# Weight units of 1024 columns in place of 512 in a two-layer diffusion trunk

## The chip, the core and the metric

The kernel runs on one core of one Trainium2 chip. The metric is the device time of one execution in microseconds, and shorter is better. The engines are named as the profile names them: PE is TensorE (matrix products), PEld its weight loads, DVE is VectorE, ACT is ScalarE, POOL is GpSimd, SP is the engine whose queue issues most DMAs here.

## What is computed

Two layers of a transformer trunk over 256 latent tokens and 256 context tokens, model width 1024. Cut to what matters:

```python
for l in range(2):
    ux = modulate(rms_norm(x, norm1_g[l]), sx1, cx1)      # same for the context h
    qa, ka, va, qb, kb, vb, pc, gates = project(ux, w_in[l], ...)
    ya = neighborhood_attention(...)   # branch a, 6 heads
    yb = gqa_block_attention(...)      # branch b, 6 query and 2 key heads, rotary
    yc = multiscale_pool(pc, ...)      # branch c
    m = ga * (ya @ w_br_a) + gb * (yb @ w_br_b) + gc * (yc @ w_br_c)
    x = x + gx1 * (m @ w_out[l])
    u2 = modulate(rms_norm(x, norm2_g[l]), sx2, cx2)
    x = x + gx2 * ((silu(u2 @ w_ff1[l]) * (u2 @ w_ff3[l])) @ w_ff2[l])   # width 2816
    # the context stream h gets the same, in the first layer only
```

The modulation vectors (`sx1`, `cx1`, ...) are products of `silu(c)` with `w_mod[l]`. All is in 32-bit floats.

## The kernel before

**Products in parts.** Each operand of a large product is held as a high and a low part, and a product is three matmuls: high by high, high by low, low by high (`mm3`, L228 to L230). A weight therefore passes three hands: a DMA on the SP queue brings it into a buffer `raw`; ACT copies it, rounded, to `wh` (L134); DVE subtracts to make `wl` (L146). PE can begin a block of products when `wh` is there and needs `wl` one or two matmuls later.

**Units.** The weights come as a list of units in the order of their use, each 128 partitions by at most `UNIT` = 512 columns: two row blocks (of 128 rows) by 256 columns, or one row block by 384 columns for the projections of branch a and of the queries of branch b. The class `Weights` keeps 7 `raw` buffers, and 6 each of `wh` and `wl` (`RAW`, `SPLIT`). When a job takes a unit (`get`), units up to 4 behind it are given to DVE to split, one more to ACT, and a DMA is issued for each `raw` buffer that a split frees.

**Special units.** 32 units of the first modulations come into slots of a general pool `gp` (68 slots of 2 KB a partition): 16 are used as they come ("whole"), 16 are split ("far"). Some jobs treat the two streams (latent, context) one after the other: the last two column pairs of `w_out` and `w_ff2` and the first pair of `w_ff1`/`w_ff3`, in layer 0. Their units are kept from the first stream for the second, with the parts in slots of `gp` ("keep"; `kept`).

**Jobs and order.** The main line is a list of jobs (`program`): first products woven with the first modulation, projections (`chunk_job`, `pool_job`), merges of the branches (`merge_job`), `w_out` and `w_ff2` (`into_job`), `ff_job`, and in the last layer `ff_first`, whose products start before the norm is known. `P`, `Q`, `N` name the pool, query and branch-a projections that open layer 1. Attention, norms and transposes are side work, woven a step at a time between steps of the main line; the later modulations are background work (`mod_bg`: DMAs to `mraw`, products summed in `macc` on DVE, L495 to L501, and for some of them on POOL, L498 and L499). A norm is: squares (`sq` on ACT, `ssq` on DVE, L520), the sum on PE (`ss`, L537, with its parts `ssh` and `ssl`), `rs` and `rstd` (L543 to L546), then `ut` (L566, L579) and its parts `uh` (ACT) and `ul` (DVE, L581). A scheduler then sets each engine's final order from dependences and program order; every engine runs its queue in order, so an instruction that waits holds all behind it.

Of the kernel before, what the change touches and what calls it, by code (L numbers as in the profile page):

```python
# [19 lines left out]
UNIT = 512  # L20
# [76 lines left out]
class Weights:  # L97
    """Weights in the order of their use: loaded far ahead, split a few units ahead."""

    RAW = 7  # L100
    SPLIT = 6
# [7 lines left out]
    def _dma(self, lim):  # L109
        while self.n_dma < min(lim, len(self.specs)):  # L110
            i = self.n_dma
            if self.specs[i][2:] in (("whole",), ("far",)):
                raw = self.slot([P, UNIT], name="whole")
            else:
                raw = self.pool.tile([P, UNIT], F32, tag="raw", bufs=self.RAW, name=f"raw{i}")
            for fill in self.specs[i][1]:
                fill(self.nc.sync, raw)
            self.raw[i] = raw
            self.n_dma += 1

    def part(self, i, tag):
        if self.specs[i][2:] == ("keep",):
            return self.slot([P, UNIT], F32R, name=tag)
        return self.pool.tile([P, UNIT], F32R, tag=tag, bufs=self.SPLIT, name=f"{tag}{i}")

# [27 lines left out]
    def whole(self, i):  # L153
        """Units that are used as they come."""
# [8 lines left out]
    def get(self, cols, held=0):  # L163
        """The next unit; `held` units before it are still to be used."""
        i = self.n_get
        self._dma(self.n_lo + self.RAW)
        self._lo(i + self.SPLIT - 1 - held)
        self._dma(self.n_lo + self.RAW)
        self._hi(min(i + self.SPLIT - held, self.n_lo + self.RAW))
# [6 lines left out]
class Trunk:  # L176
    def __init__(self, ctx, tc, a, out):
        self.nc, self.tc, self.a, self.out = tc.nc, tc, a, out
        self.cp = ctx.enter_context(tc.tile_pool(name="cp", bufs=1))
        self.gp = ctx.enter_context(tc.tile_pool(name="gp", bufs=68))  # L180
# [27 lines left out]
    def gT(self, T, name):  # L208
        """(high, low) tiles of T tokens; the two share a slot where they fit."""
# [15 lines left out]
    def mm3(self, out, st, mv, start, stop):  # L225
        """out += st.T @ mv, both operands as (high, low) parts."""
# [29 lines left out]
    def setup(self):  # L256
# [22 lines left out]
        # silu(c), silu(c_ctx) as columns, whole and in two parts  # L279
# [23 lines left out]
    def load_x(self, h):  # L303
        """Half of the channels of both streams."""
# [25 lines left out]
    def rows(self, l):  # L330
        """Per-channel vectors of a layer, turned from rows into columns."""
# [19 lines left out]
    def layer_consts(self, l):  # L351
        """Tables of a layer: rotary with the gains, relative bias, pooling weights."""
# [5 lines left out]
        tab = self.g([P, 2, 2, 2, HD], name="rope")  # q/k, tile, cos/sin  # L358
# [22 lines left out]
    def load_bias(self, l, head):  # L381
        """rpb (columns reversed) of a head: a run per query that covers its four key rows."""
# [10 lines left out]
    def mod_first(self, l, j):  # L393
        """Modulation from whole weights, four passes a product: TensorE has nothing else to do."""
# [72 lines left out]
    def mod_loads(self):  # L467
        """The weights of the jobs of mod_bg, in their order."""
# [9 lines left out]
    def mod_bg(self):  # L478
        """Modulation on VectorE: products summed over the row blocks, then over partitions."""
# [53 lines left out]
    def norm_rstd(self, c):  # L533
        """1 / rms of the tokens c, on every partition."""
# [13 lines left out]
    def need_u(self, kt, sl):  # L548
        """Emits the normed activations up to here."""
# [4 lines left out]
    def norm_u(self, kts, vs):  # L554
        """u = rmsnorm(x) * g * (1 + scale) + shift, as (high, low) parts."""
# [30 lines left out]
    def chunk_job(self, l, kind, p=0, fresh=False):  # L586
        wi = self.a["w_in"][l]
        cols = 256 if kind == "kb" else 384
        kpu = UNIT // cols
# [20 lines left out]
        def run(get):  # L610
# [12 lines left out]
            per = 2 // kpu  # L623
            for i0 in range(0, nu, per):
                ws = [get(cols, i) for i in range(per)]
                todo = [(i, k, tt) for tt in range(ntt) for i in range(per) for k in range(kpu)]
                if fresh:
                    todo.sort()
                for n, (i, k, tt) in enumerate(todo):
                    kt = (i0 + i) * kpu + k  # L630
                    step(ws[i], kt, k, tt)
                    if kt == KT - 1:
                        self.chunk_evac(l, kind, st, tt, ps[tt])
                    if n % 2 == 1:
                        yield
                if fresh and i0 + per == nu // 2:
# [55 lines left out]
    def q_stacks(self, srcs, scale):  # L692
        """Heads A and B of a pair: their (high, low) parts stacked on partitions."""
# [60 lines left out]
    def rotate(self, eng, z, nh, i, tt):  # L754
        """z (normed, nh heads) times gain, then rotary."""
# [80 lines left out]
    def pv(self, yps, y, h, n, v, pts):  # L836
        """The head's values, its (high, low) parts stacked on the stationary side, times both parts of P."""
# [108 lines left out]
    def unit(self, w, k0, nk, c0):  # L946
        """nk row blocks from k0 of 256 columns from c0."""
# [9 lines left out]
    def units(self, w, c0, nkt=KT, k0=0):  # L957
        return [self.unit(w, k0 + k, min(2, nkt - k), c0) for k in range(0, nkt, 2)]

    def kept(self, sl, specs, run):  # L960
        """A job on one stream of two: the units that the first one takes are kept for the second."""
# [15 lines left out]
    def pair(self, get, rhs, sl, ps, done, fresh=False):  # L977
        """Two column tiles of the tokens sl; done(c) as soon as tile c is complete."""
        nkt = len(rhs)
        nu = -(-nkt // 2)  # L980
        for i in range(nu):
            w = get(256)
            nk = w[0].shape[1]
            for c in range(2):
                for k in range(nk):
                    kt = 2 * i + k
                    if rhs is self.uu:
                        self.need_u(kt, sl)
                    self.mm3(
                        ps[c][:, sl],  # L990
                        [x[:, k, c * P : (c + 1) * P] for x in w],
                        [x[:, sl] for x in rhs[kt]],
                        kt == 0,
                        kt == nkt - 1,
                    )
# [516 lines left out]
```

## Time and profile before

| what | value |
|---|---|
| three runs | 1279.52, 1279.59, 1282.94 us |
| median | 1279.59 us |
| span of the profiled execution | 1281.1 us |
| PE busy | 1224.6 us, 96% |
| DVE busy | 951.9 us, 74% |
| ACT busy | 654.8 us, 51% |
| POOL busy | 315.4 us, 25% |
| moved by DMA | 185.5 MB, 145 GB/s on the mean |

The profiled execution is 1.5 us longer than the median; all places below are given in microseconds from its start. The rough map: 0 to 60 the first modulation and first products, to 180 projections and the start of attention in layer 0, to 420 attention and merges, to 500 `w_out` and the norms of the second half, to 840 the feed-forward part of layer 0, to 1080 layer 1 up to `w_out`, to the end the feed-forward part of layer 1. PE is busy nearly throughout, so what matters is the 56.5 us in which it is not, and what it waits for there.

### The profile page before, as it was taken

To read this page: it belongs to the slowest core of one execution; us is meant where nothing else is said; L and a number is where in the kernel's file an instruction comes from. 1 tells how busy PE (TensorE), PEld (TensorE's weight loads), DVE (VectorE), ACT (ScalarE), POOL (GpSimd) and SP (SyncE) were. 2 spreads that over 40 slices of the span, in tenths; PEclk is the share of its full clock that TensorE was granted. 3 is DMA by queue.
4 is the path that set the end of the run, shared out by engine and by line. 5 is a ranking of instruction groups with operands and counts; after the bars stand their busy time and mean duration, and the time that the engine had idled before them with its cause. 6 is when DMAs were issued, how large, how long until landed. Compare 5 with 4: busy or idle time off the path is not lost.

```text
span 1281.1 us, 21486 instructions
## 1 busy us (share of the span) xinstructions
PE 1224.6 (96%) x7415; PEld 1088.4 (85%) x7415; DVE 951.9 (74%) x1781; ACT 654.8 (51%) x1421; POOL 315.4 (25%) x335
## 2 busy tenths in 40 slices
PE   7999999899998979999999999989999999899998
PEld 2788888677786878888888888989999999899998
DVE  5867788998899888775555565597878878755563
ACT  4656578465432363333222333465888767654553
POOL 3252443755767530000000000067011100100000
PEclk9899999999999889999999999999999999999999
DMA  8632334434444544555455555325244466566663
GB/s 285 199 80 67 89 110 105 134 108 125 135 157 147 162 119 131 165 173 175 162 175 170 175 171 163 114 49 138 85 108 108 147 188 182 156 183 183 184 184 100
DMA packets 176137, 185.52 MB, mean 145 GB/s; under 512 B 14121, under 2 KB 149917, under 8 KB 176029
## 3 DMA queue, kind: packets, MB, share of 16 engines
q1 hardware_dynamic: 174220, 181.50, 46.5%
q0 software_dynamic: 1808, 2.66, 1.9%
q8 instruction: 58, 0.95, 0.3%
q14 instruction: 51, 0.41, 0.1%
HBM read 183.05 MB, written 1.05 MB: 144 GB/s over the span
## 4 chain that ended last, share of the span: by engine, by line
PE 73%; DVE 11%; ACT 5%; issue 4%; DMA 3%; POOL 3%; SPq 1%; DVEq 0%; ACTq 0%; POOLq 0%
PE acc L228 22%; PE acc L229 22%; PE acc L230 22%; DVE wl L146 3%; DMA whole<-in_w_mod_dram 2%; PE y L843 2%; ACT wh L134 1%; DVE macc L501 1%; DMA mraw<-in_w_mod_dram 1%; ACT p L832 1%; PE pt L889 1%; PE modt L508 1%; PE s L866 1%; DVE ptl L240 1%; POOL mt L498 1%
## 5 line engine op out<-in xcount | busy, mean ns | idle before, releaser
L134 ACT ACTIVATE wh<-raw 128x512 fp32r<-128x512 f32 (+2 forms) x512 | 307.2, 613 | 358.6 <-PE acc L229 267.0
L146 DVE TENSOR_TENSOR wl<-raw,wh 128x512 fp32r<-128x512 f32 (+2 forms) x512 | 365.7, 722 | 164.0 <-ACT wh L134 158.6
L228 PE MATMUL acc<-uh,wh 128*128 128x256 f32 (+1 forms) x1104 | 373.4, 338 | 6.4 <-DVE b L1249 3.6
L230 PE MATMUL acc<-uh,wl 128*128 128x256 f32 (+1 forms) x1104 | 369.5, 335 | 2.5 <-DVE wl L146 2.5
L229 PE MATMUL acc<-ul,wh 128*128 128x256 f32 (+1 forms) x1104 | 369.6, 335 | 0.3 <-DVE ul L581 0.3
L228 PEld LDWEIGHTS acc<-uh,wh 128*128 128x128 f32 x1104 | 211.7, 192 | 27.2 <-issue 3.8
L230 PEld LDWEIGHTS acc<-uh,wl 128*128 128x128 f32 x1104 | 211.3, 192 | 23.5 <-DVE wl L146 2.7
L229 PEld LDWEIGHTS acc<-ul,wh 128*128 128x128 f32 x1104 | 211.6, 192 | 19.8 <-DVE ul L581 0.7
L501 DVE SCALAR_TENSOR_TENSOR macc<-mraw,sf,macc 128x512 f32<-128x512 f32 x168 | 140.7, 849 | 58.7 <-DMA mraw<-in_w_mod_dram 57.8
L566 POOL TENSOR_TENSOR ut<-xT,rstd 128x256 f32<-128x256 f32 x30 | 25.2, 870 | 435.6 <-DVE rstd L546 435.5
L228 PE MATMUL acc<-wh,uh 128*128 128x384 f32 (+1 forms) x304 | 100.3, 330 | 4.6 <-ACT uh L1313 4.4
L229 PE MATMUL acc<-wl,uh 128*128 128x384 f32 (+1 forms) x304 | 98.2, 323 | 4.2 <-DVE wl L146 4.2
L230 PE MATMUL acc<-wh,ul 128*128 128x384 f32 (+1 forms) x304 | 98.7, 325 | 0.0
L499 POOL TENSOR_TENSOR macc<-macc,mt 128x512 f32<-128x512 f32 x56 | 84.3, 1506 | 3.2
L228 PE MATMUL acc<-hh,wh 128*128 128x512 f32 (+1 forms) x216 | 75.9, 352 | 0.0
L230 PE MATMUL acc<-hh,wl 128*128 128x512 f32 (+1 forms) x216 | 75.6, 350 | 0.0
L229 PE MATMUL acc<-hl,wh 128*128 128x512 f32 (+1 forms) x216 | 75.5, 350 | 0.0
L498 POOL TENSOR_SCALAR mt<-mraw,sf 128x512 f32<-128x512 f32 x56 | 63.1, 1129 | 40.6 <-DMA mraw<-in_w_mod_dram 26.5
L228 PEld LDWEIGHTS acc<-wh,uh 128*128 128x128 f32 x304 | 59.0, 194 | 6.1 <-ACT uh L1313 4.5
L229 PEld LDWEIGHTS acc<-wl,uh 128*128 128x128 f32 x304 | 59.1, 194 | 5.5 <-DVE wl L146 4.5
L832 ACT ACTIVATE p<-s,m 128x512 f32<-128x512 f32 (+1 forms) x72 | 44.3, 621 | 29.8 <-PE acc L229 8.7
L230 PEld LDWEIGHTS acc<-wh,ul 128*128 128x128 f32 x304 | 58.8, 193 | 0.6 <-DVE ul L1315 0.4
(278 smaller groups left out, 2327.5 us busy)
## 6 DMA issues: line engine op xcount, KB each, us to landing
raw<-in_w_ff_dram SPq DMA_DIRECT2D x264, 256.0 KB, 3.0
mraw<-in_w_mod_dram SPq DMA_DIRECT2D x160, 256.0 KB, 3.1
raw<-in_w_in_dram SPq DMA_DIRECT2D x112, 256.0 KB, 2.8
raw<-in_w_in_dram SPq DMA_DIRECT2D x144, 64.0 KB, 2.0
whole<-in_w_mod_dram SPq DMA_DIRECT2D x32, 256.0 KB, 5.5
raw<-in_w_out_dram SPq DMA_DIRECT2D x32, 256.0 KB, 3.0
raw<-in_w_in_dram SPq DMA_DIRECT2D x16, 192.0 KB, 2.8
raw<-in_w_br_c_dram SPq DMA_DIRECT2D x8, 256.0 KB, 2.9
```

Of the source, the lines that this page charges most:

```text
L134: self.nc.scalar.activation(hi[:, :n], self.raw[i][:, :n], AF.Copy)
L146: self.nc.vector.tensor_tensor(lo[:, :n], self.raw[i][:, :n], self.hi[i][:, :n].bitcast(F32), ALU.subtract)
L228: mm(out, st[0], mv[0], start=start, stop=False)
L229: mm(out, st[0], mv[1], start=False, stop=False)
L230: mm(out, st[1], mv[0], start=False, stop=stop)
L240: self.late.append(lambda: nc.vector.tensor_tensor(lo, src, hi.bitcast(F32), ALU.subtract))
L498: nc.gpsimd.tensor_scalar(t, w, c, 1.0, ALU.mult, ALU.mult)
L499: nc.gpsimd.tensor_tensor(acc[v], acc[v], t, ALU.add)
L501: nc.vector.scalar_tensor_tensor(acc[v], w, c, acc[v], ALU.mult, ALU.add)
L566: eng.tensor_tensor(ts[i][:, 0, :], self.xT[:, kt, c], self.r0[:, c], ALU.mult)
L832: nc.scalar.activation(pt, ps, AF.Exp, scale=-1.0, bias=m, accum_out=s[:, 0:1])
L843: mm(o, st, t[:, kt % 2, :], start=kt == 0 and i == 0, stop=kt == n - 1 and i == 1)
```

## The change

`UNIT` becomes 1024, with `RAW` = 3 and `SPLIT` = 4. A unit is now four row blocks by 256 columns, or two by 384 (768 columns; for the last row blocks of an odd count, less). Whole, far and kept units stay at 512 columns (`HALF`), since they lie in `gp` slots; the pool falls from 68 to 65 slots. `per` chooses two row blocks a unit for a job on one stream of two. `get` loses its argument `held`. Each loop walks a unit in two halves, so the order of products within a job is the same.

Columns held or under way, in units of ordinary jobs: before 7 x 512 in `raw` and 6 x 512 in parts, after 3 x 1024 and 4 x 1024. In the kept jobs, whose units stay at 512 columns, a job that takes a unit has 2 further units given to DVE instead of 4, and 3 `raw` buffers instead of 7.

```diff
-UNIT = 512
+UNIT = 1024
+HALF = UNIT // 2
...
-    RAW = 7
-    SPLIT = 6
+    RAW = 3
+    SPLIT = 4
...
-                raw = self.slot([P, UNIT], name="whole")
+                raw = self.slot([P, HALF], name="whole")
...
-            return self.slot([P, UNIT], F32R, name=tag)
+            return self.slot([P, HALF], F32R, name=tag)
...
-    def get(self, cols, held=0):
+    def get(self, cols):
         i = self.n_get
         self._dma(self.n_lo + self.RAW)
-        self._lo(i + self.SPLIT - 1 - held)
+        self._lo(i + self.SPLIT - 1)
         self._dma(self.n_lo + self.RAW)
-        self._hi(min(i + self.SPLIT - held, self.n_lo + self.RAW))
+        self._hi(min(i + self.SPLIT, self.n_lo + self.RAW))
...
-        self.gp = ctx.enter_context(tc.tile_pool(name="gp", bufs=68))
+        self.gp = ctx.enter_context(tc.tile_pool(name="gp", bufs=65))
...
-        kpu = UNIT // cols
+        kpu = {256: 4, 384: 2}[cols]
...
-            per = 2 // kpu
-            for i0 in range(0, nu, per):
-                ws = [get(cols, i) for i in range(per)]
+            for i in range(nu):
+                w = get(cols)
+                for k0 in range(0, kpu, 2):
...
-    def units(self, w, c0, nkt=KT, k0=0):
-        return [self.unit(w, k0 + k, min(2, nkt - k), c0) for k in range(0, nkt, 2)]
+    def units(self, w, c0, nkt=KT, k0=0, per=4):
+        return [self.unit(w, k0 + k, min(per, nkt - k), c0) for k in range(0, nkt, per)]
+
+    def per(self, sl):
+
+        return 4 if sl.stop - sl.start == self.tokens else 2
...
-            wu = [rows(0, 2), rows(2, 1)]
+            wu = [rows(0, 3)]
...
-        return self.kept(sl, self.units(w, jp * 256, nkt, k0), run)
+        return self.kept(sl, self.units(w, jp * 256, nkt, k0, self.per(sl)), run)
...
-            ws._dma(ws.n_whole + 4 + 2 * KT)
+            ws._dma(ws.n_whole + 2 + 2 * KT)
...
-                    ws._lo(ws.n_whole + 4)
+                    ws._lo(ws.n_whole + 2)
```

Over the whole program DVE's queue falls from 1742 to 1511 listed rows and ACT's from 1333 to 1096; PE's products are the same. Three places on DVE, where the order around a norm moves:

First pair of `w_ff1`/`w_ff3` of layer 0, latent stream, behind the norm of the context stream. Its eight kept units before are 5092, 5110, 5128, 5146, 5368, 5386, 5404 and 5448, so `wl_5448` is the eighth and last; the rows stand from the end of the first four norm steps on.

```order
L581 TENSOR_TENSOR ul_5174<-ut_5426,uh_5173 128x256
L581 TENSOR_TENSOR ul_5176<-ut_5428,uh_5175 128x256
L146 TENSOR_TENSOR wl_5448<-raw_5094,wh_5408 128x512
L579 TENSOR_SCALAR ut_5430<-ut_5430,A_111,mod_109 128x256
L579 TENSOR_SCALAR ut_5434<-ut_5434,A_111,mod_109 128x256
L581 TENSOR_TENSOR ul_5178<-ut_5430,uh_5177 128x256
L581 TENSOR_TENSOR ul_5180<-ut_5434,uh_5179 128x256
L509 TENSOR_REDUCE mod_109<-modt_5592 128x4
```

The same place of the changed kernel, where the eight units are 4744, 4762, 4984, 5002, 5020, 5064, 5096 and 5122:

```order
L582 TENSOR_TENSOR ul_4790<-ut_5042,uh_4789 128x256
L582 TENSOR_TENSOR ul_4792<-ut_5044,uh_4791 128x256
L147 TENSOR_TENSOR wl_5064<-raw_4986,wh_5024 128x512
L580 TENSOR_SCALAR ut_5046<-ut_5046,A_111,mod_109 128x256
L580 TENSOR_SCALAR ut_5050<-ut_5050,A_111,mod_109 128x256
L582 TENSOR_TENSOR ul_4794<-ut_5046,uh_4793 128x256
L582 TENSOR_TENSOR ul_4796<-ut_5050,uh_4795 128x256
L510 TENSOR_REDUCE mod_109<-modt_5208 128x4
L510 TENSOR_REDUCE mod_109<-modt_5214 128x4
L147 TENSOR_TENSOR wl_5096<-raw_5004,wh_5068 128x512
L460 TENSOR_TENSOR mod_109<-mod_109,cols_108 128x8
L147 TENSOR_TENSOR wl_5122<-raw_5022,wh_5100 128x512
```

Behind the first norm steps there is now the sixth unit of eight where there was the eighth, and the last two stand behind two reduces that wait for PE (`modt`).

Start of layer 1, DVE, at the norm of the context stream: the eight units of the `Q` job before are 8860, 8878, 8898, 8944, 8992, 9018, 9022 and 9049.

```order
L146 TENSOR_TENSOR wl_8898<-raw_8526,wh_8884 128x384
L240 TENSOR_TENSOR ssl_8835<-ssq,ssh_8834 128x256
L146 TENSOR_TENSOR wl_8944<-raw_8544,wh_8904 128x384
L543 TENSOR_SCALAR rs_8915<-ss_8912 128x256
L146 TENSOR_TENSOR wl_8992<-raw_8562,wh_8950 128x384
L545 SCALAR_TENSOR_TENSOR rs_8916<-rs_8916,rs_8915 128x256
L546 SCALAR_TENSOR_TENSOR rstd_8622<-rs_8916,rstd_8622 128x256
L146 TENSOR_TENSOR wl_9018<-raw_8580,wh_8998 128x384
L566 TENSOR_TENSOR ut_8922<-xT,rstd_8622 128x256
```

In the changed kernel the `Q` job has four units, 8140, 8170, 8256 and 8282, and 8305 is the first of the `N` job that follows:

```order
L147 TENSOR_TENSOR wl_8256<-raw_7878,wh_8176 128x768
L241 TENSOR_TENSOR ssl_8115<-ssq,ssh_8114 128x256
L147 TENSOR_TENSOR wl_8282<-raw_8142,wh_8262 128x768
L544 TENSOR_SCALAR rs_8187<-ss_8184 128x256
L546 SCALAR_TENSOR_TENSOR rs_8188<-rs_8188,rs_8187 128x256
L547 SCALAR_TENSOR_TENSOR rstd_7902<-rs_8188,rstd_7902 128x256
L147 TENSOR_TENSOR wl_8305<-raw_8172,wh_8288 128x768
L567 TENSOR_TENSOR ut_8194<-xT,rstd_7902 128x256
```

Before, six of the eight `Q` units are split ahead of the block of `ut` and `ul` (eight of these and a small split), and the last two behind it; now all of `Q` and a quarter of `N` stand ahead of it.

Last layer, `ff_first`, DVE, from the second norm's sum to the first `b` (L1249, L1258 after), which frees the accumulator that PE's next products need. Before, from the last `ut` steps on:

```order
L146 TENSOR_TENSOR wl_12705<-raw_12476,wh_12685 128x512
L581 TENSOR_TENSOR ul_12516<-ut_12595,uh_12515 128x256
L581 TENSOR_TENSOR ul_12518<-ut_12599,uh_12517 128x256
L1247 TENSOR_TENSOR ff_12642<-acc_12531,rstd_12510 128x256
L1247 TENSOR_TENSOR ff_12648<-acc_12532,rstd_12510 128x256
L1249 TENSOR_TENSOR b_12641<-b_12641,acc_12531 128x1
```

After:

```order
L147 TENSOR_TENSOR wl_11629<-raw_11457,wh_11583 128x1024
L582 TENSOR_TENSOR ul_11408<-ut_11481,uh_11407 128x256
L147 TENSOR_TENSOR wl_11661<-raw_11537,wh_11633 128x1024
L582 TENSOR_TENSOR ul_11410<-ut_11485,uh_11409 128x256
L1256 TENSOR_TENSOR ff_11522<-acc_11423,rstd_11402 128x256
L1256 TENSOR_TENSOR ff_11528<-acc_11424,rstd_11402 128x256
L582 TENSOR_TENSOR ul_11412<-ut_11496,uh_11411 128x256
L1258 TENSOR_TENSOR b_11521<-b_11521,acc_11423 128x1
```

Between `ssl` and that `b` there are four splits of 512 columns before and three of 1024 now, and one `ul` more.

## Rows read from the trace of the kernel before

**Rows 1.** Page, part 1: busy time, share of the span, instructions.

```profile
PE 1224.6 (96%) x7415; PEld 1088.4 (85%) x7415; DVE 951.9 (74%) x1781; ACT 654.8 (51%) x1421; POOL 315.4 (25%) x335
```

**Rows 2.** Stretch, length; PE, PEld, DVE, ACT, POOL busy (instructions); clock, DMA share, GB/s.

```profile
180.00:320.00 140.00, 129.72 (x697) 107.24 (x696) 128.21 (x252) 89.25 (x223) 78.51 (x71) 0.99 0.42 119
320.00:420.00 100.00, 89.70 (x406) 73.18 (x405) 88.85 (x109) 32.85 (x63) 70.68 (x53) 0.97 0.47 146
...
500.00:840.00 340.00, 340.00 (x1639) 286.38 (x1638) 215.41 (x360) 109.80 (x187) 5.99 (x8) 1.00 0.51 161
...
1080.00:1281.00 201.00, 193.99 (x1600) 193.09 (x1598) 121.11 (x219) 106.52 (x205) 5.14 (x6) 0.99 0.57 166
```

**Rows 3.** PE's waits, by releaser: us in total, times, longest.

```profile
PE pt L931 <- DVE ptl L240: 5.0, 3, 2.3
...
PE acc L229 <- DVE wl L146: 4.2, 1, 4.2
PE acc L228 <- DVE b L1249: 3.6, 1, 3.6
...
PE modt L508 <- POOL macc L499: 3.0, 1, 3.0
PE acc L229 <- DVE ml L243: 2.7, 1, 2.7
...
PE acc L230 <- DVE wl L146: 2.5, 1, 2.5
```

**Rows 4.** Page, part 5: busy, mean ns of one, idle before, its releaser.

```profile
L134 ACT ACTIVATE wh<-raw 128x512 fp32r<-128x512 f32 (+2 forms) x512 | 307.2, 613 | 358.6 <-PE acc L229 267.0
L146 DVE TENSOR_TENSOR wl<-raw,wh 128x512 fp32r<-128x512 f32 (+2 forms) x512 | 365.7, 722 | 164.0 <-ACT wh L134 158.6
```

**Rows 5.** Timeline of DVE near the start: start us, us, what, count.

```profile
31.13 1.95 DVE L146 TENSOR_TENSOR wl<-raw,wh 128x384 fp32r<-128x384 f32 x4
...
45.37 6.72 DVE L146 TENSOR_TENSOR wl<-whole,wh 128x512 fp32r<-128x512 f32 x11 [0.79 <-ACT wh L134]
```

**Rows 6.** Line L146 alone by stretch: length, DVE busy (instructions), clock, DMA share, GB/s.

```profile
180.00:320.00 140.00, 27.26 (x32) 0.99 0.42 119
320.00:420.00 100.00, 34.20 (x33) 0.97 0.47 146
...
500.00:840.00 340.00, 84.47 (x124) 1.00 0.51 161
```

**Rows 7.** Timelines of POOL and of DVE around 385.

```profile
384.69 1.60 POOL L499 TENSOR_TENSOR macc<-macc,mt 128x512 f32<-128x512 f32 x1
...
385.06 2.38 DVE L146 TENSOR_TENSOR wl<-raw,wh 128x512 fp32r<-128x512 f32 x2
```

**Rows 8.** Timelines of DVE and of PE around 480; in brackets the idle time before.

```profile
474.59 0.42 DVE L543 TENSOR_SCALAR rs<-ss 128x256 f32<-128x256 f32 x1
...
479.96 1.21 DVE L146 TENSOR_TENSOR wl<-raw,wh 128x512 fp32r<-128x512 f32 x1
...
481.22 0.54 PE L230 MATMUL acc<-uh,wl 128*128 128x256 f32 x1 [2.49 <-DVE wl L146]
```

**Rows 9.** Timelines of DVE and of PE at the start of layer 1.

```profile
849.66 1.84 DVE L566 TENSOR_TENSOR ut<-xT,rstd 128x256 f32<-128x256 f32 x2
...
858.20 2.48 DVE L146 TENSOR_TENSOR wl<-raw,wh 128x384 fp32r<-128x384 f32 x4
...
859.33 0.44 PE L229 MATMUL acc<-wl,uh 128*128 128x384 f32 x1 [4.20 <-DVE wl L146]
```

**Rows 10.** PE alone by stretch: length, busy (instructions), granted clock, DMA share, GB/s.

```profile
860.20:863.60 3.40, 3.40 (x12) 0.50 0.46 133
863.60:867.00 3.40, 3.40 (x26) 1.00 0.80 234
```

**Rows 11.** SP queue's waits (us, times, longest); a DMA issue (count, KB, us to landing).

```profile
SPq L950 <- DVE wl L146: 562.4, 324, 8.4
...
raw<-in_w_ff_dram SPq DMA_DIRECT2D x264, 256.0 KB, 3.0
```

More of the change, by code (lines that the diff above doesn't have):

```diff
@@ L621, in step @@
                 self.mm3(ps[tt][:, c0:cols], u, [x[:, k, c0:] for x in w], kt == 0, kt == KT - 1)
-            per = 2 // kpu
-            for i0 in range(0, nu, per):
-                ws = [get(cols, i) for i in range(per)]
[L626 to L636, printed above, removed]
+            for i in range(nu):
+                w = get(cols)
+                for k0 in range(0, kpu, 2):
+                    todo = [(k, tt) for tt in range(ntt) for k in (k0, k0 + 1)]
+                    if fresh:
+                        todo.sort()
+                    for n, (k, tt) in enumerate(todo):
+                        kt = i * kpu + k
+                        step(w, kt, k, tt)
+                        if kt == KT - 1:
+                            self.chunk_evac(l, kind, st, tt, ps[tt])
+                        if n % 2 == 1:
+                            yield
+                if fresh and 2 * (i + 1) == nu:
                     yield "half"
@@ L979, in pair @@
         nkt = len(rhs)
-        nu = -(-nkt // 2)
-        for i in range(nu):
+        k0 = 0
+        while k0 < nkt:
             w = get(256)
             nk = w[0].shape[1]
[L984 to L995, printed above, removed]
-                    if kt == nkt - 1:
-                        done(c)
-                    if k == nk - 1:
-                        yield
-            if fresh and i == nu // 2 - 1:
+            for k1 in range(0, nk, 2):
+                ks = range(k1, min(k1 + 2, nk))
+                for c in range(2):
+                    for k in ks:
+                        kt = k0 + k
+                        if rhs is self.uu:
+                            self.need_u(kt, sl)
+                        self.mm3(
+                            ps[c][:, sl],
+                            [x[:, k, c * P : (c + 1) * P] for x in w],
+                            [x[:, sl] for x in rhs[kt]],
+                            kt == 0,
+                            kt == nkt - 1,
+                        )
+                        if kt == nkt - 1:
+                            done(c)
+                    yield
+            k0 += nk
+            if fresh and k0 == nkt // 2:
                 yield "half"
@@ L1232, in run @@
                 for u in range(KT // 2):
-                    hi, lo = get(256)
+                    k0 = 2 * u % 4
+                    if k0 == 0:
+                        hi, lo = get(256)
                     for c in range(2):
                         cs = slice(c * P, (c + 1) * P)
-                        for k in range(2):
-                            kt = 2 * u + k
+                        for k in (k0, k0 + 1):
+                            kt = 4 * (u // 2) + k
                             xh, xl = self.plain[kt]
@@ L1291, in run @@
             yield from self.pair(get, self.uu, sl, p3, mul)
-        specs = self.units(self.a["w_ff1"][l], fp * 256) + self.units(self.a["w_ff3"][l], fp * 256)
+        per = self.per(sl)
+        specs = [u for n in ("w_ff1", "w_ff3") for u in self.units(self.a[n][l], fp * 256, per=per)]
         return self.kept(sl, specs, run)
@@ L1374, in run @@
             yield from p
-        return m0[0] + m2[0] + wa[:4] + m1[0] + m3[0] + wp[:2] + wa[4:] + wp[2:], run
+        return m0[0] + m2[0] + wa[:2] + m1[0] + m3[0] + wp[:1] + wa[2:] + wp[1:], run
     def in_order(self):
```

## The prediction

> **What bounds the kernel now.** The first view is the busy table: PE works 1224.6 of 1281.1 us [rows 1], so 56.5 us at most can be won, unless the products themselves run slower. DVE is next with 951.9. The second view cuts the span into stretches [rows 2]. From 500 to 840 PE never stops, with DVE at 215 of 340: whatever the change saves there on DVE or ACT buys nothing. From 180 to 420 it is another picture: DVE has 128.2 of 140 and 88.9 of 100 us, and PE stands still for 10.3 + 10.3 = 20.6. The third view tells for whom PE waits [rows 3]. The large single waits all end with DVE or with something that POOL or DVE holds up: two with a weight's low part (4.2 and 2.5), one each with `b`, `macc` and `ml`, three with `ptl`. None ends with a weight's DMA. So the weights' way is bound neither by DMA nor by ACT, whose copies mostly wait for PE to free a buffer (267.0 of 358.6 us of idle time before them [rows 4]). What decides is when DVE comes to a split, and what a split holds up on DVE's queue.
>
> **Sizes.** Eleven splits of 512 columns in a row take 6.72 us, 0.61 each, and four of 384 take 1.95, 0.49 each [rows 5]. The difference is 0.12 us for 128 columns, so one of 1024 should take 0.61 + 4 x 0.12 = 1.1; double the small one is 1.22. I take 1.16, an estimate between the two, and a saving of 0.06 (0 to 0.12) a pair. With some 240 pairs that is about 14 us of DVE's 952, most of it where PE is never short. ACT's copies save likewise, and nobody waits for them: I put that at nothing. Its cover is ACT's idle time; a copy that comes late would cost the rest of its 0.61.
>
> **Start, to 54 us: +1.2.** Sixteen far units are split one by one under the first products; the last eleven run back to back [rows 5], and the products behind them wait for DVE. When PE ends the first projection's rows, each of its units gives a split buffer back. Four units of 384 columns gave four, and five far units were split by then, eleven left; two units of 768 give two, and by the order of the changed kernel three are split, thirteen left. Two more come late: 2 x 0.61. Bounds 0 (the DMA covers it) and 1.8.
>
> **Attention and merges, 180 to 420: -3.** The 65 splits of these two stretches become about 33. Against 84.47 / 124 = 0.68 us a split in the quiet stretch they take 27.26 for 32 and 34.20 for 33 [rows 6], that is 5.5 and 11.7 us too long. The cause is to be seen at 385: POOL's sum runs from 384.69 to 386.29, and of two splits begun at 385.06, which should take 1.3, the pair takes 2.38 [rows 7]; the first ends some 0.55 us behind POOL's instruction. DVE waited for POOL's instruction to end. If that happens once an instruction, half as many splits wait half as often: 17.2 / 2 = 8.6, with 32 x 0.06 = 1.9 of fixed cost 10.5 us of DVE. Of that PE gets what lies before one of its waits; the single wait that is plainly of this kind is the one for `macc`, 3.0 [rows 3], so I take 3. The bounds: -10.5, and +3, if a split of 1.16 in front of `ptl` or `ksl` delays them each time by half a split, 0.55, at half a dozen places. One such place I count by itself: the last merge, where one longer split stands before `ml`: **+0.5** (0 to 1.1).
>
> The Trainium skill (SBUF — State Buffer, Who interferes with whom) says of a DVE tensor_tensor with both inputs in SBUF that it shares a read port with GpSimd, and that the one that issues first keeps it for its whole instruction. The rows at 385 agree. By that rule the saving on DVE would come in full, 1270 instead of 1277 below; but it also says that a POOL instruction behind a split is blocked for as long as the split lasts, and a split of 1024 lasts twice as long.
>
> **`w_out` in layer 0, 420 to 456: -0.6.** Of the splits between the first pairs' residual and the norm's `ssl` one fewer (0.6) stands before it on DVE, and PE waits for that norm in any case. Bounds -1.5 and +2, since only two kept units are ready behind the one in use.
>
> **First pair of the feed-forward part, 466 to 486: +1.** A kept unit is 12 products, at 193.99 / 1600 = 0.12 us [rows 2] 1.45 us of PE. Before, the seventh unit was split ahead of the norm's chain, which DVE works through from 474.59 to 479.96 (5.4 us), and the eighth's split came right behind: PE waited 2.49 for it [rows 8]. The order now has five units ahead of that chain. PE runs dry two units earlier, 2.9 us; against that, DVE reaches the chain 1 to 2 us sooner, since six splits for the pair that follows and two or three kept ones no longer stand before it, and the first products of the other stream can fill in behind the sixth unit. 2.9 - 1.5 - 0.4 gives +1. Bounds 0 and +5.7: two more waits of 2.0 each and the clock, below.
>
> **Start of layer 1, 842 to 877: -3.** Six of eight units of `Q` were split ahead of the block of `ut` and `ul` (849.66 to 858.20, 8.5 us), the other two behind it, and PE waited 4.20 [rows 9]. Behind that wait PE ran 3.4 us with a granted clock of 0.50, 12 products where the next 3.4 us at 1.00 took 26 [rows 10]: 1.2 GHz in place of 2.4, a loss of 1.7. After, all of `Q` and the first unit of `N` stand ahead of the block, so both go: -5.9. But this first unit of `N` needs a buffer that PE frees only when it is through with the first unit of `Q`, and DVE's whole queue, the block with it, waits there: An estimate of the delay: the 12 products of that unit (at 3.4 / 26 = 0.13 us or a little more [rows 10], near 2), then a copy and a split of 768 columns (0.9 each) lie between the end of the pool job and the block, 3.8 us, where DVE came to the block about 1 us behind that end: some 2.9 us for the norm of the context stream, which the later products of `N` use. So -5.9 + 2.9 = -3. Bounds -5.9 and +1.
>
> **`ff_first`, 1079 to 1096: +1.4.** PE waits 3.62 for `b` [rows 3], which frees its accumulator. Between `ssl` and `b` stood 4 x 0.61 = 2.4 and now stand 3 x 1.16 = 3.5 and one more `ul` of 0.3. Bounds +0.5 and +2.
>
> **At nothing.** From 500 to 840 and from 1100 on the ring of three `raw` buffers has to keep up. One unit of 1024 is 24 products, 2.9 us at the 256 tokens of the last layer, three are 8.7. One turn of a buffer is a DMA, a copy and a split: 3.0 us is the landing time of 256 KB [rows 11]; twice that, 6.0, is the upper bound for 512, with 1.2 and 1.2 it is 8.4. It fits, by 0.3 at worst; at 340 / 1639 = 0.21 a product in layer 0 [rows 2] by over 6. The 562 us that the SP queue waits for splits [rows 11] are waits for free buffers and become fewer and longer. The three lost slots of `gp` show no price in any row; 0, and at worst one wait like the 3.0 above.
>
> **The sum.** 1.2 - 3 + 0.5 - 0.6 + 1 - 3 + 1.4 = -2.5. On the profiled span that is 1278.6 of 1281.1; the span lies 1.5 above the median, and the median becomes 1279.6 - 2.5 = 1277.1. That is -0.2%; a measurement of this kernel can tell about 0.3%, 3.8 us, from no change.
>
> **The rivals.** *Relief*: DVE's 10.5 us in 180 to 420 all reach PE, since DVE is over 90% busy there: 7.5 more than in the sum, 1269.6. For it speaks that PE's idle 20.6 us lie just there; against it, that PE is short there for single results, in front of which a longer split now stands. *Short look-ahead*, the slower one: in kept jobs two units ready are 2.9 us of PE, four were 5.8, and DVE's chain of a norm takes 5.4 [rows 8]. Four just cover it, two cannot; it decides as soon as DVE doesn't come to the chain earlier by the difference. Then the feed-forward pair costs 5.7 instead of 1 and `w_out` 2 instead of -0.6: 1277.1 + 7.3 = 1284.4, and 1287.4 if layer 1 gains nothing. *Nothing reaches PE*: the units change, PE's waits are for other things and only shift: 1279.6. *The ring starves PE*: if a turn takes 1 us over the 8.7, the last layer's 64 feed-forward units, 21 turns, cost 21 us: 1298.
>
> **How the numbers follow.** The forecast 0.42 (its own range 1273 to 1281, so 0.15 of it faster, 0.27 within 0.3%); relief 0.24 (0.23 faster, 0.01 within); short look-ahead 0.20 (0.19 slower, 0.01 within); nothing 0.11 (0.09 within, 0.01 on either side); the ring 0.03, slower. Faster 0.39, same 0.38, slower 0.23. The range reaches from relief with its unsure half microsecond, 1269, to the far end of the short look-ahead, 1287; the ring and a little at both ends stay out.
>
> **What would show it.** Splits of 1024 at about 1.16 us, and those from 180 to 420 together well under 61.5 us; at 859 no wait of PE, but a later block of `ut`; at 481 a wait that begins earlier, at the sixth unit; at 1095 a wait of some 5 us for `b`; from 500 to 840 PE at 340. The prediction is wrong if PE waits for `wh` or a `raw` DMA in the feed-forward parts, if PE's idle time from 180 to 420 moves by more than 6 us, or if new waits of 3 us and more, with their half clock, stand between 420 and 500.

## The result, and the profile after

The changed kernel takes 1297.55 us on the median (1295.81 to 1298.92, four runs) against 1280.92 for the kernel before on the same chip: a ratio of 1.0119 (95% interval 1.0098 to 1.0139). It is **slower by some 15 us**; 1277.1, within 1269 to 1287, was forecast. The profiled execution took 1295.81 us, with a span (first to last instruction) of 1293.9 where before had 1281.1. A span is some 1.9 us shorter than the time of the same execution, so the profiled execution of the kernel before must be the one of 1282.94, the longest of its four; that of the changed kernel was the shortest of its four.

Page of the changed kernel, part 1 (columns as in [rows 1]), then part 5 for the splits and copies (as [rows 4]):

```profile
PE 1225.5 (95%) x7415; PEld 1088.1 (84%) x7415; DVE 912.4 (71%) x1545; ACT 617.5 (48%) x1185; POOL 322.4 (25%) x335
...
L147 DVE TENSOR_TENSOR wl<-raw,wh 128x1024 fp32r<-128x1024 f32 (+2 forms) x276 | 319.2, 1159 | 189.4 <-ACT wh L135 185.1
L135 ACT ACTIVATE wh<-raw 128x1024 fp32r<-128x1024 f32 (+2 forms) x276 | 264.3, 961 | 318.6 <-PE acc L230 144.3
```

DVE has 40 us less to do and ACT 37 less, PE as much as before, and still it stands 12 us longer: 68.4 in place of 56.5. The waits of PE, which answer to [rows 3]:

```profile
PE acc L231 <- DVE wl L147: 10.7, 7, 5.2
PE acc L229 <- DVE b L1258: 7.7, 2, 7.5
PE ss L538 <- ACT ssh L239: 4.4, 2, 2.3
...
PE acc L229 <- DVE v L241: 4.0, 4, 1.6
...
PE pt L932 <- DVE ptl L241: 2.1, 3, 1.0
```

The waits for weights' low parts grow from 6.7 to 10.7 and the one for `b` from 3.6 to 7.5; those for `ptl` shrink.

**Where the time went.** The 2088 groups of three products on the main line come in the same order in both kernels, but for four near 110 us that change places. So the start of each can be taken from both traces and subtracted: how far the changed kernel lags (+) or leads (-) at that product. Worked out so, at the time of the product in the kernel before, for the changed kernel and some of the experiments below ("halves" is the changed kernel with each copy and split made in two):

```
before    changed   5 raw   4 raw  7 raw  halves  5 raw + halves
   61.1     +1.1    +1.1    +0.5   -1.7    +1.2     +0.3
  179.6     +2.5    +2.4    +1.9   -0.3    +1.0     -0.2
  320.0     +2.6    +3.2    +0.9   +3.1    +1.1     +0.4
  395.3     -4.2    -3.1    -5.9   -3.2    -2.9     -0.9
  430.3     -4.9    -2.7    -6.1   -4.1    -2.3     -2.4
  456.2     -4.7    -5.8    -8.1   -6.1    -3.0     -4.8
  515.3     +2.1    -4.8    -6.7   -2.1    +1.6     -2.5
  820.2     +2.1    -4.8    -6.7   -2.1    +1.6     -2.5
  845.3     +6.1    -4.1    -3.5   +2.3    +7.3     -2.2
  864.3     -0.0    -7.2    -5.8   -0.2    +3.1     -5.8
  877.2     +6.0    -7.0    -4.7   +0.6    +4.4     -5.7
 1068.3     +8.7    -2.1    -0.4   +2.4    +5.1     -3.4
 1095.3    +12.3    +1.5    +3.4   +6.0    +4.9     -3.6
 1270.3    +12.6    +2.0    +4.2   +6.3    +4.9     -3.6
```

Read down the second column: to 430 the change has won 5 us. Then it loses 6.8 at the first feed-forward pair (456 to 515), 4.0 at the last pairs of `w_ff2` in layer 0 (820 to 845), and 3.6 in `ff_first` (1068 to 1095). At the start of layer 1 it wins 6.1 and loses 6.0 again. Elsewhere the column stands still: from 515 to 820 to a hundredth.

What the loss at the feed-forward pair is made of stands in the chain of waits of the changed kernel from 466 (start, us, what):

```profile
466.71 0.70 DVE wl L147
467.41 0.02 SPq L951
467.43 0.03 issue
467.46 4.75 DMA raw<-in_w_ff_dram
472.21 0.02 issue
472.23 0.63 ACT wh L135
472.87 0.32 ACT rs L545
```

A split ends and frees a `raw` buffer; only then can the load of the unit three further on be issued. It lands 4.75 us later. ACT, which works its queue in order, has come to the copy of that unit and waits, and behind the copy stands `rs`, a step of the context stream's norm that needs no weight at all. The timelines of ACT and of PE show the same from their side (in brackets the idle time before):

```profile
468.46 0.47 ACT L543 ACTIVATE rstd<-ss,eps 128x256 f32<-128x256 f32 x1 [1.08 <-PE ss L540]
472.23 0.63 ACT L135 ACTIVATE wh<-raw 128x512 fp32r<-128x512 f32 x1 [3.29 <-DMA raw<-in_w_ff_dram]
472.77 0.40 ACT L545 ACTIVATE rs<-rstd 128x256 f32<-128x256 f32 x1
...
479.79 0.58 PE L231 MATMUL acc<-uh,wl 128*128 128x256 f32 x1 [5.16 <-DVE wl L147]
```

So DVE's chain of `ut` and `ul` starts at 474.1, the sixth unit's split behind it comes at 478.5, and PE waits 5.16 us for it.

From 820 to 845 the chain is of the same kind. Here the loads that come late are one of the kept units and two of the next layer's first weights, and what stands behind the copy is `ssh`, the first part of the next norm's sum:

```profile
818.94 4.57 DMA raw<-in_w_ff_dram
823.53 0.64 ACT wh L135
...
826.30 4.74 DMA raw<-in_w_in_dram
831.14 1.07 ACT wh L135
...
833.49 3.24 DMA raw<-in_w_in_dram
836.83 0.84 ACT wh L135
837.67 0.32 ACT ssh L239
```

Over the whole run ACT's copies wait so for loads (the view of ACT's waits: sum in us, times, the longest):

```profile
ACT wh L135 <- DMA raw<-in_w_ff_dram: 18.0, 10, 3.4
...
ACT wh L135 <- DMA raw<-in_w_in_dram: 12.5, 7, 3.0
...
ACT wh L135 <- DMA raw<-in_w_out_dram: 4.3, 2, 2.9
```

Before, the same waits were 2.6 us for `w_ff` and 12.4 for `w_in`, none for `w_out`.

### The profile page after: what moved, and what is told of

It reads as the page before. It is cut to its first block, busy times and chain, and to the rows that moved or that the text cites. A ratio compares the mean times of both kernels' runs of the same rounds, so it can differ in the third digit from the quotient of the medians.

```text
span 1293.9 us, 20052 instructions
## 1 busy us (share of the span) xinstructions
PE 1225.5 (95%) x7415; PEld 1088.1 (84%) x7415; DVE 912.4 (71%) x1545; ACT 617.5 (48%) x1185; POOL 322.4 (25%) x335
## 4 chain that ended last, share of the span: by engine, by line
PE 60%; DVE 14%; ACT 7%; POOL 6%; issue 6%; DMA 6%; SPq 1%; DVEq 0%; ACTq 0%; POOLq 0%
PE acc L229 18%; PE acc L230 18%; PE acc L231 18%; DVE wl L147 4%; DMA mraw<-in_w_mod_dram 2%; ACT wh L135 2%; ACT p L833 2%; DVE macc L502 2%; POOL macc L500 2%; POOL mt L499 1%; ACT p L835 1%; DMA raw<-in_w_ff_dram 1%; PE y L844 1%; DMA raw<-in_w_in_dram 1%; DMA whole<-in_w_mod_dram 1%
## 5 line engine op out<-in xcount | busy, mean ns | idle before, releaser
L147 DVE TENSOR_TENSOR wl<-raw,wh 128x1024 fp32r<-128x1024 f32 (+2 forms) x276 | 319.2, 1159 | 189.4 <-ACT wh L135 185.1
L135 ACT ACTIVATE wh<-raw 128x1024 fp32r<-128x1024 f32 (+2 forms) x276 | 264.3, 961 | 318.6 <-PE acc L230 144.3
```

The costliest lines, as they stand in the source:

```text
L135: self.nc.scalar.activation(hi[:, :n], self.raw[i][:, :n], AF.Copy)
L147: self.nc.vector.tensor_tensor(lo[:, :n], self.raw[i][:, :n], self.hi[i][:, :n].bitcast(F32), ALU.subtract)
```

## The experiments

The first theory, after the traces: **the ring of loads**. In the jobs on one stream a `raw` buffer holds a unit of 512 columns as before, but there are three and not seven. Its rivals: **split buffers** (four of each part; ACT's copies wait for PE to free one), **length** (a copy or split of 1024 columns holds up twice as long what stands behind it), and **slots** (65 for 68).

**Five raw buffers.**

```diff
-    RAW = 3
+    RAW = 5
...
-        self.gp = ctx.enter_context(tc.tile_pool(name="gp", bufs=65))
+        self.gp = ctx.enter_context(tc.tile_pool(name="gp", bufs=61))
```

> The changed kernel with five raw buffers in place of three (pool of slots 61 in place of 65). Theory ring: in the jobs whose units stay at 512 columns three raw buffers hold only three small loads, ACT waits for the landing and the norm's small operations wait behind it on ACT; of 13 us lost there (435 to 449, 456 to 490, 820 to 840) some 10 come back: about 1287. Theory split buffers (ACT's copies wait for PE to free one of four): no more than 2 us come back, about 1295. Theory slots: 61 slots are worse than 65, over 1297.

Measured: 1284.79 us, ratio 1.0007 to the kernel before (0.9990 to 1.0025). The losses from 456 to 515 (6.8) and from 820 to 845 (4.0) are gone (+1.0 and +0.7), and ACT's waits for loads fall to 1.3 us for `w_ff` and 3.5 for `w_in`, with none for `w_out`. At the start of layer 1 the 6.0 from 864 to 877 are gone too (+0.2). In the feed-forward pair the copies now run in one piece and `rs` follows `rstd` at once:

```profile
463.97 1.65 ACT L135 ACTIVATE wh<-raw 128x512 fp32r<-128x512 f32 x3
466.52 0.47 ACT L543 ACTIVATE rstd<-ss,eps 128x256 f32<-128x256 f32 x1 [0.89 <-PE ss L540]
467.02 0.42 ACT L545 ACTIVATE rs<-rstd 128x256 f32<-128x256 f32 x1
```

The look-ahead of the splits is still two kept units here: it was the loads, not the splits, that were too few. One thing moved besides: in ACT's queue the third of these copies stands in front of `rstd`, where the changed kernel has it between `rstd` and `rs`. What the earlier load and what this order gives was not separated. `b` still costs 7.5.

**Five buffers for each part.** `SPLIT` = 5, 61 slots, three `raw` buffers.

```diff
-    SPLIT = 4
+    SPLIT = 5
```

> The changed kernel with five buffers for each part in place of four (61 slots in place of 65). Theory split buffers: the late start of the pool branch at the start of layer 1 (7.9 us lost from 865 to 878) and the wait for b in the last layer (3.9 more) shrink, 6 to 8 us together: about 1289. Theory ring: kept jobs as slow as before since they are held by raw; 1293 to 1297. Theory slots: over 1297.

Measured: 1300.23, ratio 1.0132 (1.0103 to 1.0161). No gain: `b` is still 7.5, and from 864 to 877 4.6 us are still lost in the trace. The theory of the split buffers falls. More splits ahead with the same three loads even lost at the start (+4.7 at 61 us): a copy waits 3.61 us for a load, and `mrow`, a row of the modulation behind it on ACT, comes late, so PE waits 5.6; the chain is the same as at 472.

**Loads of 1024 columns in the kept jobs too,** parts in two slots each:

```diff
+class Halves: ...          # row block k of a unit whose part lies in two slots
...
-        return 4 if sl.stop - sl.start == self.tokens else 2
+        return 4
```

> The changed kernel, but jobs on one stream of two also load units of 1024 columns (one raw buffer, one DMA), whose parts lie in two slots each; buffers and slots as in the changed kernel. Theory ring: as with five raw buffers, some 10 of the 13 us of the kept jobs come back: about 1287, and ACT's waits for raw from 430 to 480 mostly gone. Theory split buffers: at most 2 us, 1295. Theory length of a split: the parts are still made in pieces of 512, so nothing changes there, 1297.

Measured: 1287.20, ratio 1.0030 (1.0012 to 1.0048). Another cure, with three buffers and as many slots as the changed kernel, gives back some 10 us, but only in part where it was expected. From 430 to 515 the trace still loses 3.6 (the changed kernel 7.0, five buffers none) and from 820 to 845 1.1: 6.3 of the 10.6 us in the trace come from the kept jobs, the others from the start of layer 1 (3.2) and from before 430.

**61 slots and nothing else.**

```diff
-        self.gp = ctx.enter_context(tc.tile_pool(name="gp", bufs=65))
+        self.gp = ctx.enter_context(tc.tile_pool(name="gp", bufs=61))
```

> The changed kernel with 61 slots in place of 65 and nothing else, the control for the two with more buffers. Theories ring and split buffers: no difference beyond 2 us, 1295 to 1299. Theory slots (part of the loss comes from 65 in place of 68): 4 to 8 us slower, 1301 to 1305.

Measured: 1296.28, ratio 1.0101 (1.0086 to 1.0117). In its trace ACT and DVE run the same instructions in the same order as in the changed kernel. Slots cost nothing at this number, and the two runs with more buffers may be read without them.

**Copies and splits in halves,** five raw buffers; loads and buffers stay whole.

```diff
-            self.nc.scalar.activation(hi[:, :n], self.raw[i][:, :n], AF.Copy)
+            for o in range(0, n, n if n <= HALF else n // 2):
+                e = o + (n if n <= HALF else n // 2)
+                self.nc.scalar.activation(hi[:, o:e], self.raw[i][:, o:e], AF.Copy)
```

(the same for the split on DVE)

> The kernel with five raw buffers, loads and buffers of 1024 columns, but each copy and each split made as two instructions of half the columns. Theory length of an instruction: in the last layer the wait for b falls from 7.5 back to about 3.6 (two long splits and the copy that waits for a buffer no longer stand in one piece before the norm), 3 to 4 us less there; and in 180 to 420, where the longer splits wait for GpSimd half as often, the 5 us that the five-buffer kernel gains on the kernel before go. Sum about 1284 to 1286. Theory buffers (the wait for b comes from a buffer that is freed a whole unit at a time): b stays at 7.5, and nothing changes in 180 to 420 either.

Measured: 1280.01, ratio 0.9980 (0.9963 to 0.9996), less than expected by 4 us and the first to be faster than the kernel before. The wait for `b`:

```profile
PE acc L233 <- DVE b L1262: 3.4, 1, 3.4
```

With the same buffers 7.5 became 3.4: the loss in `ff_first` comes from the length of the instructions, of copies and splits together; the two were not tried apart. The timelines of DVE show it, first of the changed kernel, from `ssl` to `b`:

```profile
1093.52 0.42 DVE L241 TENSOR_TENSOR ssl<-ssq,ssh 128x256 fp32r<-128x256 f32 x1
1095.38 1.23 DVE L147 TENSOR_TENSOR wl<-raw,wh 128x1024 fp32r<-128x1024 f32 x1 [1.45 <-ACT wh L135]
1096.52 0.42 DVE L544 TENSOR_SCALAR rs<-ss 128x256 f32<-128x256 f32 x1
...
1103.47 1.21 DVE L147 TENSOR_TENSOR wl<-raw,wh 128x1024 fp32r<-128x1024 f32 x1
...
1104.94 1.21 DVE L147 TENSOR_TENSOR wl<-raw,wh 128x1024 fp32r<-128x1024 f32 x1
...
1107.41 0.21 DVE L1258 TENSOR_TENSOR b<-b,acc 128x1 f32<-128x1 f32 x2
```

and with halves:

```profile
1080.67 0.41 DVE L245 TENSOR_TENSOR ssl<-ssq,ssh 128x256 fp32r<-128x256 f32 x1
1081.01 0.68 DVE L151 TENSOR_TENSOR wl<-raw,wh 128x512 fp32r<-128x512 f32 x1
1082.11 0.43 DVE L548 TENSOR_SCALAR rs<-ss 128x256 f32<-128x256 f32 x1 [0.43 <-ACT rstd L547]
...
1091.52 0.14 DVE L1262 TENSOR_TENSOR b<-b,acc 128x1 f32<-128x1 f32 x1
```

13.9 us from `ssl` to `b` against 10.9 (the kernel before: 11.5). The other side: from 179.6 to 395.3 the five-buffer kernel won 5.5 us with whole splits and wins 0.7 with halves, as expected.

**Seven raw buffers** (`RAW` = 7, 57 slots).

> The changed kernel with seven raw buffers (57 slots). Theory ring: the kept jobs already had nearly all back with five; 0 to 2 us more than with five, 1283 to 1285. Theory slots: 57 slots begin to bind, over 1287.

Measured: 1291.65, ratio 1.0076 (1.0051 to 1.0102); against expectation slower than with five. The loss is in the kept jobs again (+4.0 from 456 to 515, +4.4 from 820 to 845). See the run with 57 slots below.

**Five raw buffers and loads of 1024 in the kept jobs** (both edits above).

> Five raw buffers (61 slots) and loads of 1024 columns also in the jobs on one stream. If both cure the same loss (theory ring) the two together give no more than the better one, 1283 to 1286; if they cure two different ones (rival: the size of the ring, and the number of loads in it), the gains add and it ends at 1277 to 1280.

Measured: 1287.72, ratio 1.0046 (1.0031 to 1.0062). The gains don't add, as the theory said, but the size was missed: it is slower than five buffers alone (1.0007, 0.9990 to 1.0025). In the trace it loses 4.3 us from 430 to 515, where five buffers alone win 2.1. The larger loads bring back the pattern of 472: a copy waits for a load, `ssh` of a norm stands behind it on ACT, and PE waits 6.6 us for that.

```profile
452.74 1.06 ACT L147 ACTIVATE wh<-raw 128x1024 fp32r<-128x1024 f32 x1 [2.59 <-DMA raw<-in_w_ff_dram]
453.70 0.40 ACT L259 ACTIVATE ssh<-ssq 128x256 fp32r<-128x256 f32 x1
```

So the run speaks against two losses that are cured apart, but it is no clean proof of one.

**The kernel before with four raw buffers.**

```diff
-    RAW = 7
+    RAW = 4
```

> The kernel before with four raw buffers of 512 columns in place of seven, split buffers and slots as they were: the ring alone, without longer units. Theory ring: ACT waits for raw in the kept jobs, whose norms come late; 4 to 10 us slower, 1286 to 1292. Theory look-ahead of the splits (the rival of the prediction): the six split buffers still allow four units ahead, so nothing changes, within 2 us of 1281.

Measured: 1288.85, ratio 1.0053 (1.0030 to 1.0077). The size was hit, the place was not: in the trace 3.9 us are lost by 61 us and 6.1 from 180 to 395, 7.6 are won back from 395 to 515, and at the end the lag is 5.5. The kept jobs lose only 1.4, from 820 to 845. At the start the mechanism is the one of 472, with another victim, `mrow` of the modulation (ACT's timeline):

```profile
55.42 0.52 ACT L134 ACTIVATE wh<-raw 128x384 fp32r<-128x384 f32 x1 [2.69 <-DMA raw<-in_w_in_dram]
55.85 0.57 ACT L435 ACTIVATE mrow<-mod 4x512 f32<-4x512 f32 x1
```

PE waits 3.7 us for that row. ACT's copies wait 24.2 us for `w_ff` loads here (20 times), more than the 18.0 of the changed kernel, and yet the feed-forward pair loses nothing: such a wait costs PE only where something that PE needs soon stands behind the copy.

**Four raw buffers in the changed kernel** (`RAW` = 4, 63 slots).

> The changed kernel with four raw buffers (63 slots). Theory ring: a load takes about 3 us to land and a kept unit is used in 1.5 to 2.8 us, so a fourth buffer gives back most of what five did: 1286 to 1290, and ACT's waits for raw in the feed-forward and w_out weights about half of the changed kernel's 22 us. Rival, that the fifth buffer and not the fourth matters, or that the gain came from another order of the program: 1293 or more.

Measured: 1284.45, ratio 1.0016 (1.0003 to 1.0029), as good as five; ACT's waits for `w_ff` and `w_out` loads are 7.5 and 1.9. In the total the fourth buffer is the one that counts. By places it is so in the feed-forward pair (+1.4 from 456 to 515, where three buffers lose 6.8), but from 820 to 845 four still lose 3.2 of the 4.0; there it takes the fifth (+0.7).

**Five raw buffers, 57 slots.**

> Five raw buffers and 57 slots, as the kernel with seven raw buffers had. Theory slots: it is as slow as that one (1289 to 1292), with the loss against 61 slots in the kept jobs, whose parts lie in those slots (470 to 490 and 820 to 845). Theory too many loads ahead: it stays at 1284 to 1286, as with 61 slots.

Measured: 1287.46, ratio 1.0039 (1.0025 to 1.0053), between the two expectations: against 61 slots (1.0007) 57 cost some 0.3%. Where, the trace doesn't show, as the profiled execution was the fastest of the ten (1283.85). In it nothing is lost in the kept jobs (-5.4 at 456, -4.7 at 515, -4.2 at 845). So 57 slots don't explain what seven raw buffers lose there. The trace of that kernel has single waits of PE for splits there (3.2 and 2.6 us) and of ACT for loads (up to 2.0 in the feed-forward pair, one of 4.8 for `w_in` between 815 and 850); whether loads further ahead hold up the nearer ones, or only the order came out otherwise, was not tried and stays open.

**Whole copies and splits in the merges of layer 0 only,** halves elsewhere, five raw buffers.

```diff
+        specs = self.units(a["w_in"][l], gate0 + jp * 256) + wu
+        return [s + ("long",) for s in specs] if l == 0 else specs, run
```

> Five raw buffers, 61 slots, copies and splits of half a unit everywhere but in the merges of layer 0, where they stay whole. Theory: whole splits pay where DVE shares its time with GpSimd (320 to 395, where the kernel with whole splits gained 3.8 us and that with halves 1.3) and cost where a norm or a transposition waits behind them; so 2 to 3 us less than with halves everywhere, 1277 to 1278. Rival: the gain of 320 to 395 is given back before 500, where DVE is late anyway: 1280.

Measured: 1279.57, ratio 0.9974 (0.9960 to 0.9988): with halves everywhere it was 0.9980, and the intervals cover each other. In the trace -6.4 at 395, but -3.9 at 430 and -3.5 at 515: what the whole splits win is mostly given back before 515. The rival was right. It has the lowest ratio of all versions, 0.26% below the kernel before, though it can't be told from halves everywhere.

**Halves with three raw buffers**, the fourth corner.

> The changed kernel (three raw buffers, 65 slots), each copy and split made as two instructions of half the columns. Theory two causes that add (ring, length of an instruction): the wait for b falls to about 3.6 and the start is 2 us better, as with five buffers and halves, but the kept jobs stay as slow as in the changed kernel, with ACT's waits for raw near 20 us for the feed-forward and w_out weights; 5 to 6 us less than the changed kernel, 1290 to 1293. Theory one cause (long instructions alone hold up ACT and DVE, the ring only through them): 1280 to 1284.

Measured: 1289.32, ratio 1.0055 (1.0037 to 1.0073), a microsecond better than expected. ACT still waits 18.3 us for `w_ff` loads, `b` is at 3.4, and from 820 to 845 5.7 us are lost, where the changed kernel lost 4.0. In the feed-forward pair halves alone already save some: +4.6 from 456 to 515 in place of 6.8. With the last lags of the table the four corners are: 12.6 changed, 2.0 with five buffers, 4.9 with halves, -3.6 with both. Five buffers give 10.6 and 8.5, halves 7.7 and 5.6: two causes that nearly add. By the measured ratios five buffers give 1.12% and 0.75%, halves 0.64% and 0.27%, and both together 1.39% where the sum would be 1.76: they overlap in part.

## Why the prediction was wrong

**The step that failed** is "At nothing", together with the sentence that nobody waits for ACT's copies. The ring of three buffers was sized there with units of 1024 columns, and for those the verdict holds: from 515 to 820 the lag doesn't move. But the kept units stay at 512, and for them the change takes four of seven loads away. A turn of such a buffer is a load, a copy and a split of 0.6 each; three units are 3 x 1.45 = 4.4 us of PE. With the 3.0 us of [rows 11] the turn is 4.2 and would just have fitted, so that sum, which was not made, would have shown a cover of 0.2 us and no more; with the 4.75 us of the load at 467.46 the turn is 5.95 and does not fit. Five `raw` buffers took the losses in the kept jobs away, and ACT's waits for `w_ff` and `w_out` loads fell from 22.3 to 1.3 us. The second half of the error is where the lateness lands: "a copy that comes late would cost the rest of its 0.61" is wrong, since ACT waits in its queue's order, and `rs`, `ssh` or `mrow` behind the copy is late by as long as the copy waits for its load (3.29 us at 472). The sign that the prediction itself named, a new wait of 3 us or more between 420 and 500, came: 5.16.

**Point by point**, by the lag's steps:

- Start, +1.2: measured +1.1. Thirteen far splits in a row take 7.94 us (45.12 on) where [rows 5] had eleven in 6.72. Right, by the step.
- 180 to 420, -3, the last merge +0.5: measured -7.4 from 180 to 430. Right in sign, and in cause for about half of it. The splits there take 22.12 + 27.24 = 49.4 us against 61.5 in [rows 6], 12.1 less where 10.5 was worked out; with halves and three buffers, as many splits as before, they take 28.72 + 32.56 = 61.3 again (the changed kernel first, then halves; columns as in [rows 6]):

```profile
180.00:320.00 140.00, 22.12 (x18) 0.99 0.41 117
320.00:420.00 100.00, 27.24 (x17) 0.97 0.44 141
...
180.00:320.00 140.00, 28.72 (x35) 0.98 0.42 117
320.00:420.00 100.00, 32.56 (x32) 0.97 0.43 141
```

But halves still win 3.3 of the 7.4 (2.3 with five buffers, where whole splits win 5.1). So the longer splits, which wait less often for POOL, are worth some 3 to 4 us of PE, near the 3 of the forecast and far from the 10.5 of *relief*; what wins the others was not followed. The Trainium skill's rule on the shared port (SBUF — State Buffer, Who interferes with whom) agrees with the 49.4 and 61.3.
- `w_out`, -0.6: measured +0.2 from 430 to 456, though by another way: 3.5 lost to late loads by 448, 3.3 won at the norm.
- Feed-forward pair, +1, with 5.7 as the bound: measured +6.8. The rival *short look-ahead* named the place and nearly the price, but not the cause: five raw buffers, with the same two splits ahead, bring it to +1.0, the number of the forecast. The term was right for what it priced; the late load was missing in it.
- The last pairs of `w_ff2`, 820 to 845: no term; measured +4.0. They are kept jobs too, and were not looked at; no large wait of PE stood there in the trace before. The chain at 820 shows the cause of `rs` again, with `ssh` behind the copies.
- Start of layer 1, -3: measured -0.1 in all, -6.1 and then +6.0. The wait of [rows 9] and its half clock are gone, within 0.2 us of the -5.9 forecast. What comes late next was misjudged: not the norm, but the pool branch, whose evacuation stands on ACT behind two copies that wait for buffers (`vp` at 861.0, some 6 us behind its products), so PE waits 2.41 for `plh` and runs at half clock for 6.7 us after it (PE's timeline, then a stretch of PE: length, busy, granted clock, DMA share, GB/s):

```profile
868.84 0.58 PE L229 MATMUL pool<-plh,wpoolh 128*128 128x256 f32 x1 [2.41 <-ACT plh L239]
...
868.40:875.10 6.70, 6.26 (x23) 0.50 0.59 185
```

Half of 6.7 and the 2.41 make 5.8 of the 6.0. More buffers for the parts don't cure it (4.6 still lost), while five and four `raw` buffers leave 0.2 and 1.1; with five, `vp` stands ahead of those copies in ACT's queue.
- `ff_first`, +1.4: measured +3.6. Right cause, too small. Two whole splits where the sum counted one more microsecond, and the copy in front of `rstd`, which waits for a buffer that is only freed a unit at a time: the 1.45 us ahead of the split at 1095.38 was not in the sum.
- 60 to 180 and 877 to 1068, no terms: +1.4 and +2.7. With halves they are -0.5 and +2.3 (five buffers), so the first goes with the length of the instructions again, and the second was not settled.

The terms add up to 12.6 in the traces. The medians lie 16.6 apart; the profiled execution of the changed kernel took the least time of its four, that of the kernel before the most of its four, and what lies between has no place in any trace.

## What to carry to other kernels

When a unit of work grows and the buffers become fewer, look for the places where the unit does not grow: there the ring has shrunk by the whole factor. On an engine that works in order, price a late operand by what is queued behind the instruction that waits for it, not by that instruction. And size of transfer, size of buffer and size of instruction are three choices: here large loads in five buffers, with instructions of half a unit, did better than either kernel, by 0.2% against the one before.

## What the runs showed of the hardware

A load of 512 KB lands in 3.7 us where one of 256 KB took 3.0 [rows 11]; the Trainium skill (SBUF — State Buffer, The DMA setup-cost knee) gives about 2 us and bytes by 436 GB/s, an estimate of 3.2 and 2.6, so the step of 0.6 agrees with the 0.7 here while the measured times lie 0.5 and 0.4 above. Bandwidth was not short where a load came late: in the 4.75 us of the load at 467.46 the DMA engines were busy 0.56 of the time and moved 165 GB/s.

A split of 1024 columns takes 1.14 us in a row of them (two: 2.35) and one of 512 0.6, so the saving of merging two in a row was 0.06 us, as estimated. A split that starts on an idle DVE takes 1.22 and 0.69, so that there a pair saves 0.16: from 500 to 840, where POOL does next to nothing, DVE's splits fell from 84.47 to 75.99 us without any gain for PE. Between 180 and 420 fewer waits for POOL come on top.
